# Low-rank gate products in fours on the column groups, activations held until the fourth

## The chip, the cores and the metric

The kernel runs as one program on one core of a Trainium2 chip. Its metric is device time in microseconds (us). PE is the matrix engine (TensorE) and PEld its weight loads; DVE, ACT and POOL are VectorE, ScalarE and GpSimd; SPq is the queue of SyncE, which issues most DMA transfers here.

## The reference

One layer of a diffusion backbone on 128 prompt tokens and 1024 latent tokens, D = 1024. Cut to what matters here:

```python
h = rmsnorm(x, norm1) * (1 + scale1) + shift1
q_a, k_a, v_a, g_a, lr_a, q_b, f_b, i_b, g_b = jnp.split(h @ w_in, offsets, axis=-1)
lr = lr_a.reshape(B, T, 2, GLA_LOWRANK)  # 2 x 16 = 32 of the columns of w_in
alpha_logit = jnp.einsum('btdr,drk->dbtk', lr, w_gla_up) + b_gla[:, None, None, :]
log_alpha = jax.nn.log_sigmoid(alpha_logit.astype(jnp.float32)) / GLA_GATE_NORM
```

The mixer's gated scans with `log_alpha`, its output product and a convolutional FFN follow.

## The kernel before, in words

The 1152 tokens are cut into three blocks `g` of 384 (three tiles of 128 tokens each, `xt`), taken in the order 2, 1, 0. The 1024 columns are cut into eight blocks `kt` of 128. For each `g` and `kt` the function `modulate` does this:

- three transposes on PE (L478) bring the normalised tokens into a PSUM tile `x`; there are four such tiles, in the pools `ps_o` and `ps_lv`;
- one operation takes it out of PSUM with scale and shift into the SBUF tile `tt`: on DVE (L487), or on ACT (L483) for blocks 2 and 5 of `g` 1 and 0;
- ACT makes the rounded half `h1h` (L492), POOL (even `kt`) or DVE (odd `kt`) the remainder `h1l` (L69);
- the hook `each`, here `lr_part` (L528), multiplies `tt` by the 32 low-rank columns `wlr`. Such a product fills 32 of the array's 128 columns. Its place among the four column groups, and so the 32 PSUM partitions of `plr` that it writes, is `kt % 4`.

`modulate` is called with `kt` 0 to 3 and then 4 to 7, so a block `g` has two sets of four low-rank products; the second set accumulates onto the first. The trace records each of the 24 products as two matmuls. After both calls ACT takes `plr` out (L555) and stores it in DRAM as `scr_lr`, from where a later stage loads it again as `lr` (L835) for the products with `wup` (L839).

Before a block's transposes, `norm_x` normalises each of its three tiles: a sum of squares on ACT (L378), two small steps on DVE and POOL (L379, L380), and a scaling of the tile on DVE (L385). After a block's `modulate` come projections of 24 matmuls each (L506), called here by output and block: q of block 2; k of 2 and q of 1; k of 1, q and k of 0. Then the next stage begins with L839 and the projections at L617.

The order of each engine's instructions is not written by hand here. The program is built with a scheduler that lists the instructions of an engine by its own estimate of when each is ready, and at run time each engine takes them strictly in that order. `tc.issue_after(i)` tells that scheduler to put what follows behind instruction `i`. So a change in one place can move instructions on every engine near it. Pools hand out buffers in turn: the sixth `tt` waits until the first is free.

Of the kernel before, what the change touches and what calls it, by code (L numbers as in the profile page):

```python
# [49 lines left out]
def kernel(ctx: ExitStack, tc: tile.TileContext, ins, outs, stop=None):  # L50
# [3 lines left out]
    def pool(stack, name, bufs, space=None, side=None):  # L54
        kw = {} if space is None else {"space": space}
        if side is not None:
            kw["side"] = side
        return stack.enter_context(tc.tile_pool(name=name, bufs=bufs, reuse_waits="tile", **kw))

    mm = nc.tensor.matmul  # L60
# [203 lines left out]
    def next_w():  # L264
        prefetch_w()
        while pos["used"] in stored:
            pos["used"] += 1
            prefetch_w()
        pos["used"] += 1
        return pos["got"][pos["used"] - 1]  # L270
# [22 lines left out]
    es0 = ExitStack()  # L293
    rowp = pool(es0, "rows", 1)
    wap_ = pool(es0, "wa", 12)
    xp = pool(es0, "x", 3)
    tp = pool(es0, "t", 5)

    crow = rowp.tile([16, P], F32, name="crow")
    nc.sync.dma_start(crow[0:8, :], ins["c_ctx"].rearrange("(k p) -> k p", p=P))  # L300
# [82 lines left out]
    def norm_x(t):  # L383
        st = rstd_of(tp, x_in[t], "p")
        nc.vector.tensor_scalar(x_in[t], x_in[t], st[:, 1:2], None, op0=ALU.mult)  # L385
# [3 lines left out]
    for i in range(2):  # L389
        nc.vector.memset(modA[i], 0.0)  # L390
        t = modA[i][:, :]
# [7 lines left out]
    for i in range(2):  # L399
        ps = (ps_a, ps_mm)[i].tile([2 * 32, 512], F32, name="ada", tag=("ada", "mm")[i])  # L400
        psA.append(ps)
        for kt in range(KT):
# [4 lines left out]
            for j in range(2):  # L407
# [4 lines left out]
                    start=(kt == 0),  # L412
                    stop=(kt == KT - 1),
                    skip_group_check=True,
# [9 lines left out]
    wlr = rowp.tile([P, KT, 32], F32, name="wlr")  # L424
# [14 lines left out]
    def ada_first(i):  # L439
        nc.vector.tensor_tensor(modA[i], psA[i], modA[i], op=ALU.add)  # L440
        pt = ps_x.tile([P, 4, P], F32, name="x", tag="x")
        for q in range(4):
            nc.tensor.transpose(pt[:, q, 0:64], modA[i][:, q * P : (q + 1) * P], ident[0:64, 0:64])
        nc.vector.tensor_copy(b1[i], pt[:, :, 0:2])
        for v in range(2):
            nc.vector.scalar_tensor_tensor(
                s1[i][:, :, v],
                pt[:, :, 32 + v],
                one_c[:, 0:1],
                vcol[:, col["norm1"] + 4 * i : col["norm1"] + 4 * i + 4],  # L450
                op0=ALU.add,
                op1=ALU.mult,
            )
# [18 lines left out]
    def modulate(g, xns, s, b, hi, lo, psum, tpool, lo_eng, each=None, t_act=(), kts=range(KT)):  # L472

        for kt in kts:
            pool_, tag = psum[kt % len(psum)]
            pt = pool_.tile([P, BL], F32, name="x", tag=tag)
            for i in range(3):
                nc.tensor.transpose(pt[:, i * P : (i + 1) * P], xns[i][:, kt * P : (kt + 1) * P], ident)  # L478
            t = tpool.tile([P, BL], F32, name="tt", tag="tt")
            parts = [(0, BL, 1)] if g < 2 else [(0, 2 * P, 1), (2 * P, BL, 0)]  # L480
            for c0, c1, v in parts:
                if kt in t_act:
                    nc.scalar.activation(  # L483
                        t[:, c0:c1], pt[:, c0:c1], AF.Identity, scale=s(kt, v), bias=b(kt, v)
                    )
                    continue
                nc.vector.tensor_scalar(  # L487
                    t[:, c0:c1], pt[:, c0:c1], s(kt, v), b(kt, v), op0=ALU.mult, op1=ALU.add
                )
            h_, l_ = hi(kt, g), lo(kt, g)  # L490
            for (c0, c1, hp_), (_, _, lp_) in zip(h_, l_):
                nc.scalar.activation(hp_, t[:, c0:c1], AF.Copy)  # L492
                split_lo(lo_eng[kt % len(lo_eng)], lp_, t[:, c0:c1], hp_)
            if each is not None:
                each(kt, t)
# [3 lines left out]
    def proj_d(w, b):  # L499

        hi, lo = w
        ps = ps_mm.tile([P, BL], F32, name="mm", tag="mm")
        n = 0
        for kt in range(KT):
            for a, h in ((hi, h1h), (hi, h1l), (lo, h1h)):
                mm(ps, a[:, kt, :], h[kt][b], start=(n == 0), stop=(n == 23))  # L506
                n += 1
        return ps
# [4 lines left out]
    def evac(ps, nm, scale=1.0):  # L513
        t = new_pj(nm)
        nc.scalar.activation(t, ps, AF.Copy, scale=scale)  # L515
        return t

    first_q, first_k = {}, {}
    for g in (2, 1, 0):
        if g < 2:  # L520
            for t in range(3 * g, 3 * g + 3):
                norm_x(t)
        xns = [x_in[t] for t in range(3 * g, 3 * g + 3)]
        plr = ps_mm.tile([P, BL], F32, name="mm", tag="mm")

        def lr_part(kt, t):
            j = kt % 4
            mm(  # L528
                plr[32 * j : 32 * j + 32, :],
                wlr[:, kt, :],  # L530
                t,
                start=(kt < 4),
                stop=(kt >= 4),
                skip_group_check=True,
            )

        for i in range(2):
            if g == 2 and i == 1:
                ada_first(1)
            modulate(  # L540
                g,
                xns,
                lambda k, v: s1[k // 4][:, k % 4, v : v + 1],
                lambda k, v: b1[k // 4][:, k % 4, v : v + 1],
                lambda k, g: [(0, BL, h1h[k][g])],
                lambda k, g: [(0, BL, h1l[k][g])],
                ((ps_o, "o"), (ps_lv, "lv")),
                tp,
                (nc.vector,) if g == 2 and i == 0 else (nc.gpsimd, nc.vector),
                lr_part,  # L550
                (1, 3, 5) if g == 2 else (2, 5),
                range(4 * i, 4 * i + 4),
            )
        lrs = tp.tile([P, BL], F32, name="lrs", tag="lrs", bufs=1)
        nc.scalar.activation(lrs, plr, AF.Copy)  # L555
        nc.scalar.dma_start(scr_lr[g], lrs)
        if g == 2:
            wq = next_w()
            first_q[2] = evac(proj_d(wq, 2), "qj", 0.125)
            wk = next_w()  # L560
        elif g == 1:
            first_k[2] = evac(proj_d(wk, 2), "kj")
            first_q[1] = evac(proj_d(wq, 1), "qj", 0.125)
        else:
            first_k[1] = evac(proj_d(wk, 1), "kj")
            first_q[0] = evac(proj_d(wq, 0), "qj", 0.125)
            first_k[0] = evac(proj_d(wk, 0), "kj")
# [637 lines left out]
    for n, u in enumerate(groups):  # L1205
# [7 lines left out]
        for bi, b in enumerate(ORDER):  # L1213
            fb, k, k0 = ready
            lv = levels(u, b, fb, k, k0)
            for slot in range(8):
                at = 8 * bi + slot
                last = anchor["mm"] = next(lv)
# [1095 lines left out]
def build(nc, shapes, outs_kind="ExternalOutput", stop=None):  # L2314
    ins = {
        n: nc.dram_tensor(f"in_{n}_dram", s, dt, kind="ExternalInput").ap() for n, (s, dt) in shapes.items()
    }
    outs = [
        nc.dram_tensor(f"out_{i}_dram", s, F32, kind="ExternalOutput").ap() for i, (s, _) in enumerate(_OUTS)
    ]  # L2320
    with tile.TileContext(nc, schedule_with_timeline_sim=True) as tc:
        kernel(tc, ins, outs, stop)
# [14 lines left out]
```

## Time and profile before

| | |
|---|---|
| median of 3 runs | 1548.68 us (1547.78 to 1554.11) |
| profiled execution, its own time | 1549.85 us |
| its span, first to last instruction | 1548.1 us |
| PE busy | 1487.8 us (96%), 12506 matmuls |
| DVE, ACT, POOL busy | 1145.5 us (74%), 783.2 us (51%), 708.9 us (46%) |
| low-rank products, L528 | 48 records, first at 31.7 us, last at 72.7 us |
| granted TensorE clock | 0.99 mean |

The change lies in the first 90 us of the span, so shares of the whole span say little about it. The chain of work that ended last, listed in order of time, tells which engine the end of that stretch hangs on; a timeline gives the single instructions, and a view by stretches the busy time of each engine in a window.

### The profile page before, as it was taken

Reading aid. Unit: us, or ns where it says so; the run is one execution under the profiler, and the core shown is the slowest. Engines: PE = TensorE matmul, PEld = TensorE weight load, DVE = VectorE, ACT = ScalarE, POOL = GpSimd, SP = SyncE. Lnnn points to the kernel's source line nnn. Section 1 sums busy time; section 2 is a strip of 40 time slices with the busy share of each in tenths; the row PEclk is TensorE's granted clock in tenths of the full one; section 3 lists DMA queues with packets and bytes.
Section 4 is the critical chain, followed back from the end, with each engine's and each line's share of the span. In section 5 each row is a group of like instructions: output and inputs, shape, how many; then the busy total and the mean of one; then the engine's idle time right before and its main releaser. Section 6 shows DMA issues by size and latency. Waiting matters only on the chain.

```text
span 1548.1 us, 31132 instructions
## 1 busy us (share of the span) xinstructions
PE 1487.8 (96%) x12506; PEld 1255.0 (81%) x12506; DVE 1145.5 (74%) x1731; ACT 783.2 (51%) x1523; POOL 708.9 (46%) x538
## 2 busy tenths in 40 slices
PE   7999999999999989899989999999999999999997
PEld 2699998999898978777767888888888887788886
DVE  3657466664556757655789999999999999579575
ACT  3566567555454544512664444444444444467444
POOL 1412122334233240222227999999999996000001
PEclk9999999999999999999999999999999999999999
DMA  9311121335435362677652555545644666879752
GB/s 339 113 54 47 35 65 51 120 92 189 135 123 182 111 198 80 235 272 278 200 180 77 179 166 128 136 118 146 193 117 135 179 162 200 330 244 360 245 192 115
DMA packets 172940, 252.49 MB, mean 163 GB/s; under 512 B 11733, under 2 KB 113603, under 8 KB 170875
## 3 DMA queue, kind: packets, MB, share of 16 engines
q1 hardware_dynamic: 149591, 172.21, 34.8%
q0 software_dynamic: 22592, 77.60, 16.2%
q8 instruction: 98, 1.61, 0.4%
q10 hardware_dynamic: 611, 0.68, 0.1%
q14 instruction: 48, 0.39, 0.1%
HBM read 190.62 MB, written 82.90 MB: 177 GB/s over the span
## 4 chain that ended last, share of the span: by engine, by line
PE 78%; DMA 6%; DVE 6%; issue 4%; ACT 3%; POOL 2%; SPq 1%; POOLq 0%; ACTq 0%; DVEq 0%
PE u L1742 26%; PE mm L603 13%; PE xb L2199 6%; PE yb L2199 6%; PE mm L617 5%; PE x L1970 4%; PE mm L746 3%; PE lv L935 3%; PE yb L2250 2%; PE u L1512 2%; DVE acc L1906 2%; PE x L1003 1%; PE mm L506 1%; DMA mh<-scr_m 1%; DMA wa<-in_w_ada_dram 1%
## 5 line engine op out<-in xcount | busy, mean ns | idle before, releaser
L1906 DVE SCALAR_TENSOR_TENSOR acc<-u,convc,acc 128x945 f32<-128x945 f32 (+2 forms) x352 | 426.8, 1218 | 7.8 <-ACT acc L1894 0.7
L69 POOL TENSOR_TENSOR wl<-raw,wh 128x1024 fp32r<-128x1024 f32 x42 | 103.6, 2468 | 241.0 <-ACT wh L132 183.2
L603 PE MATMUL mm<-h1h,wh 128*128 128x384 f32 x528 | 186.0, 352 | 0.8 <-ACT qj L515 0.8
L603 PE MATMUL mm<-h1l,wh 128*128 128x384 f32 x528 | 180.0, 341 | 0.0
L603 PE MATMUL mm<-h1h,wl 128*128 128x384 f32 x528 | 180.0, 341 | 0.0
L898 DVE TENSOR_TENSOR Q<-Q,fb 128x384 f32<-128x384 f32 x126 | 86.3, 685 | 90.5 <-PE lv L935 89.0
L69 POOL TENSOR_TENSOR wul<-sr,wuh 128x512 fp32r<-128x512 f32 (+1 forms) x64 | 116.2, 1816 | 19.5 <-ACT wuh L1727 19.3
L69 POOL TENSOR_TENSOR wul<-ra,wuh 128x1024 fp32r<-128x1024 f32 x44 | 112.3, 2552 | 20.3 <-ACT wuh L1727 17.8
L888 ACT ACTIVATE m<-k 128x384 f32<-128x384 f32 x126 | 70.2, 557 | 86.9 <-PE lv L935 39.8
L2174 POOL TENSOR_TENSOR sq<-sq,mhalf 128x1 f32<-128x1 f32 x9 | 11.1, 1231 | 213.3 <-DVE sq L2171 213.3
L603 PEld LDWEIGHTS mm<-h1h,wh 128*128 128x128 f32 x528 | 100.3, 190 | 5.7 <-issue 3.9
L603 PEld LDWEIGHTS mm<-h1l,wh 128*128 128x128 f32 x528 | 100.3, 190 | 0.6 <-issue 0.2
L603 PEld LDWEIGHTS mm<-h1h,wl 128*128 128x128 f32 x528 | 100.0, 189 | 0.8 <-issue 0.5
L617 PE MATMUL mm<-wh,h1h 128*128 128x256 f32 x288 | 83.9, 291 | 0.8 <-ACT v L642 0.8
L900 DVE TENSOR_TENSOR k<-k,fb 128x384 f32<-128x384 f32 x126 | 74.2, 589 | 12.2 <-ACT m L888 6.7
L617 PE MATMUL mm<-wh,h1l 128*128 128x256 f32 x288 | 80.5, 280 | 0.0
L617 PE MATMUL mm<-wl,h1h 128*128 128x256 f32 x288 | 80.4, 279 | 0.0
L132 ACT ACTIVATE wh<-raw 128x1024 fp32r<-128x1024 f32 x50 | 53.0, 1059 | 44.0 <-PE mm L603 11.3
L2002 POOL TENSOR_TENSOR acc<-acc,acc 128x1152 f32<-128x1152 f32 x22 | 60.0, 2729 | 9.8 <-DVE acc L1906 9.8
L1727 ACT ACTIVATE wuh<-ra 128x1024 fp32r<-128x1024 f32 x42 | 44.3, 1055 | 39.5 <-issue 16.6
L1934 ACT ACTIVATE u2p<-u 128x512 f32<-128x512 f32 x44 | 26.4, 601 | 70.1 <-PE u L1742 70.1
L1727 ACT ACTIVATE wuh<-sr 128x512 fp32r<-128x512 f32 (+1 forms) x62 | 48.1, 775 | 24.1 <-PE x L1970 16.1
(387 smaller groups left out, 4485.5 us busy)
## 6 DMA issues: line engine op xcount, KB each, us to landing
ra<-in_w_ffn_up_dram SPq DMA_DIRECT2D x84, 256.0 KB, 3.0
raw<-in_w_in_dram SPq DMA_DIRECT2D x32, 512.0 KB, 4.7
v<-in_w_ada_dram SPq DMA_DIRECT2D x27, 512.0 KB, 4.3
scr_g<-acc POOLq DMA_DIRECT2D x22, 576.0 KB, 5.4
scr_s<-late POOLq DMA_DIRECT2D x11, 1024.0 KB, 5.9
scr_t<-in_w_ffn_down_dram POOLq DMA_DIRECT2D x16, 704.0 KB, 7.2
wa<-in_w_ada_dram SPq DMA_DIRECT2D x16, 512.0 KB, 6.2
scr_t<-in_w_ffn_down_dram POOLq DMA_DIRECT2D x2, 2816.0 KB, 13.5
```

The source lines that it names most:

```text
L69: return eng.tensor_tensor(out, full, hi.bitcast(F32), op=ALU.subtract)
L603: anchor["fill"] = mm(ps, a[:, kt, :], h[kt][b], start=(n == 0), stop=(n == 23))
L617: anchor["fill"] = mm(ps, h[kt][t // 3][:, ts_], a[:, kt % 4, :], start=(n == 0), stop=(n == 23))
L888: nc.scalar.activation(aps(t, 0, [[2 * h, NB], [h, 2], [1, h]]), aps(src, 0, [[2 * h, NB], [BL + h, 2], [1, h]]), AF.Copy)
L898: nc.vector.tensor_tensor(qm, qm, aps(ff_, 2 * h - 1, [[BL - h, 2], [2 * h, NB], [0, h]]), op=ALU.mult)
L900: nc.vector.tensor_tensor(km, km, aps(ff_, BL + 2 * h - 1, [[-(BL + h), 2], [2 * h, NB], [0, h]]), op=ALU.mult)
L1727: first = nc.scalar.activation(hi, raw, AF.Copy)
L1742: last = mm(dst, w_slot(c, a, x)[:, kt, :], HB[y][b][:, kt, :], start=(start and n == 0), stop=(stop and n == 11), skip_group_check=True,)
L1906: last = nc.vector.scalar_tensor_tensor(o, u3[:, r0 + dy : r1 + dy, c0 + dx : c1 + dx], wc(3 * (dy + 1) + dx + 1), o, op0=ALU.mult, op1=AL ...
L1970: last = mm(pk, HB[h]["p"][:, 4 * half + kt, :], aps(flat(W[x]), a * 512 + kt * P, [[(b - a) * 512, 2], [1, P]]), start=(half + kt + n == ...
L2002: last = nc.gpsimd.tensor_tensor(accg, accg, accu, op=ALU.mult)
L2199: anchor["down"] = mm(banks[i], w[a][:, ts_], w[b][:, 512:1024], start=(start and j == 0 and n == 0), stop=(j == NPAIR - 1 and n == 2), sk ...
```

## The change

`lr_part` no longer issues its product at once. It keeps `(kt, tt)` in a list, and when the fourth is there it issues all four, the last one first, each ordered behind the one before it. All four `tt` of a set now stay in use until then, and the pool `t` gets 7 buffers for its tiles instead of 5.

```diff
-    tp = pool(es0, "t", 5)
+    tp = pool(es0, "t", 7)
...
+        parts_lr = []
+
         def lr_part(kt, t):
-            j = kt % 4
-            mm(
-                plr[32 * j : 32 * j + 32, :],
-                wlr[:, kt, :],
-                t,
-                start=(kt < 4),
-                stop=(kt >= 4),
-                skip_group_check=True,
-            )
+            parts_lr.append((kt, t))
+            if len(parts_lr) < 4:
+                return
+            last = None
+            while parts_lr:
+                kt, t = parts_lr.pop()
+                j = kt % 4
+                with tc.issue_after(last.ins) if last is not None else nullcontext():
+                    last = mm(
+                        plr[32 * j : 32 * j + 32, :],
+                        wlr[:, kt, :],
+                        t,
+                        start=(kt < 4),
+                        stop=(kt >= 4),
+                        skip_group_check=True,
+                    )
```

Each engine runs the same instructions as before, and from the first L839 on PE, and the matching places of the other engines, they stand in the same order. Line numbers behind the edit are 9 higher: the low-rank product is L528 before and L537 after.

In the rows that follow, a number behind a name is that of a buffer: `h1h_366` to `h1h_387` are block 2 (the eight `kt` in steps of three), `h1h_365` to `_386` block 1, `h1h_364` to `_385` block 0. The first place is PE between the end of the projection q of block 2 and the start of k of block 2, where the first set of block 1 begins.

```order
 L506 MATMUL mm<-h1h_387,wl 128x384
-L478 MATMUL x<-ident,xt 128x128 x8
-L528 MATMUL mm<-tt,wlr 32x384
+L478 MATMUL x<-ident,xt 128x128 x13
+L537 MATMUL mm<-tt,wlr 32x384 x4
 L478 MATMUL x<-ident,xt 128x128 x3
 L506 MATMUL mm<-h1h_366,wh 128x384
```

The first set of block 1 now goes out at once, behind the transposes of seven of the block's eight `kt`; the other three products, and nine transposes, have left the stream of k that follows.

The second place is PE between k of block 2 and q of block 1.

```order
 L506 MATMUL mm<-h1h_387,wl 128x384
-L528 MATMUL mm<-tt,wlr 32x384
-L478 MATMUL x<-ident,xt 128x128 x2
-L528 MATMUL mm<-tt,wlr 32x384
-L478 MATMUL x<-ident,xt 128x128 x4
+L478 MATMUL x<-ident,xt 128x128 x6
+L537 MATMUL mm<-tt,wlr 32x384 x4
+L478 MATMUL x<-ident,xt 128x128 x6
 L506 MATMUL mm<-h1h_365,wh 128x384
```

The second set of block 1 stands here as a four, among the twelve transposes for the first four `kt` of block 0, and no longer reaches into the stream of q. The first set of block 0, a four before too, stands between q and k of block 1; its second set, three issues within k before, is one four behind it.

The third place is DVE around the first set of block 1, with the normalisation of tiles of blocks 1 and 0 (L379, L385) and the copies out of PSUM for the first set (L487).

```order
-L379 TENSOR_SCALAR st<-st 128x1
+L379 TENSOR_SCALAR st<-st 128x1 x2
+L385 TENSOR_SCALAR xt<-xt,st 128x1024
 L69 TENSOR_TENSOR h1l_411<-tt,h1h_387 128x384
 L379 TENSOR_SCALAR st<-st 128x1
 L385 TENSOR_SCALAR xt<-xt,st 128x1024 x2
-L379 TENSOR_SCALAR st<-st 128x1 x2
-L487 TENSOR_SCALAR tt<-x,s_0_340,b_0_342 128x384 x2
+L379 TENSOR_SCALAR st<-st 128x1
+L487 TENSOR_SCALAR tt<-x,s_0_340,b_0_342 128x384 x3
 L385 TENSOR_SCALAR xt<-xt,st 128x1024
```

One scaling of a tile has moved ahead of the remainder `h1l` and of the copies, and the set's three copies on DVE now follow each other with no scaling between them. On SP's queue the load of `wup` (L817 before, L826 after) has moved from ahead of five `xt` loads to behind the first two loads of states (L827), with the `lr` loads behind it.

## The prediction

> **What bounds the kernel now.** I read the chain that ended last first, as shares.
>
> ```profile
> PE 78%; DMA 6%; DVE 6%; issue 4%; ACT 3%; POOL 2%; SPq 1%; POOLq 0%; ACTq 0%; DVEq 0%
> ```
>
> PE carries 78% of the end, but the edit touches only 31 to 73 us of 1548, so I went on to the same chain in order of time there. Columns: start, time on the chain, what. Nine of the single products (`x2`, two records each) stand between 50.08 and 72.40; the first and the last of them are shown.
>
> ```profile
> 45.44 0.69 DVE tt L487
> 46.13 0.04 issue
> 46.17 0.83 PE mm L528 x2
> 47.01 0.48 PE x L478 x3
> 47.48 2.60 PE mm L506 x15
> 50.08 0.76 PE mm L528 x2
> ...
> 64.69 0.87 PE x L478 x8
> 65.56 0.78 PE mm L528 x8
> 66.34 0.48 PE x L478 x3
> ...
> 71.08 0.77 PE mm L528 x4
> 71.85 0.55 PE mm L506 x2
> 72.40 0.76 PE mm L528 x2
> 73.16 9.18 PE mm L506 x51
> 82.34 1.29 PE o L839 x4
> ```
>
> From 46.17 on every piece is PE, and nothing but PE. The busy time of that stretch says the same (length, then PE, PEld, DVE, ACT, POOL, granted clock, DMA, GB/s):
>
> ```profile
> 46.17:82.18 36.01, 36.01 (x188) 25.78 (x189) 18.28 (x28) 14.54 (x28) 14.85 (x12) 1.00 0.17 52
> ```
>
> PE is busy all 36.01 us at full clock, DVE for 18.28. So work taken off PE here comes off the end, as long as PE finds its inputs.
>
> **The low-rank products.** A product alone costs 0.76 us of chain (`x2`), two together 0.77 (`x4`), four together 0.78 (`x8`): four on four column groups run side by side. Between 46.17 and 73.16 the chain pays 12 slots: 0.83 + 9 x 0.76 + 0.77 + 0.78 = 9.22 us. The change leaves four fours, 4 x 0.78 = 3.12. That is **-6.1 us**. Both sets of block 2, earlier, are fours already. The fours now go out last column group first; I take their price as unchanged.
>
> The Trainium skill (TensorE: Matmul & The Clock Gate, Part 3, Measured speedup vs the span model) speaks for less: three column tiles were measured at 2.38 times one, not 3. At that efficiency of 0.79 a four would be an estimated 0.96 us and the term -5.4, the time 1543.5. Here the trace shows 0.78, and the measurement decides.
>
> **Entering and leaving.** A product among projections costs more than its slot:
>
> ```profile
> 61.72 0.34 PE L506 MATMUL mm<-h1l,wh 128*128 128x384 f32 x1
> 61.99 0.83 PE L528 MATMUL mm<-tt,wlr 128*32 128x384 f32 x2
> 62.75 0.45 PE L506 MATMUL mm<-h1h,wl 128*128 128x384 f32 x1
> 63.03 0.34 PE L506 MATMUL mm<-h1h,wh 128*128 128x384 f32 x1
> ```
>
> Projection matmuls start 0.17 us apart (2.60 / 15), but here it is 0.27 before the product and 0.28 after it: 0.2 us for one visit. Eight visits fewer are worth 0 (if transposes at the same places still pay it) to -1.6; the transposes too now come in longer runs, so I take the middle, **-0.8 us**.
>
> **First set of block 1.** PE must now hold its queue until the fourth `tt` is there, with the last transposes and the whole of k of block 2 behind it. The copies in question before, from DVE's and ACT's timelines:
>
> ```profile
> 45.44 1.26 DVE L487 TENSOR_SCALAR tt<-x,s,b 128x384 f32<-128x384 f32 x2 [0.30 <-PE x L478]
> 46.62 0.74 DVE L385 TENSOR_SCALAR xt<-xt,st 128x1024 f32<-128x1024 f32 x1
> 47.28 0.67 DVE L487 TENSOR_SCALAR tt<-x,s,b 128x384 f32<-128x384 f32 x1
> 45.94 0.66 ACT L483 ACTIVATE tt<-x,b,s 128x384 f32<-128x384 f32 x1
> ```
>
> ACT's copy is ready at 46.6 and no limit. DVE now does three copies in a row, 3 x 0.63 = 1.9, from 45.44, or up to 0.74 later for the scaling that moved ahead: done at 47.3 to 48.1. The four adds 0.78 and three transposes 0.33 (0.11 each, 0.87 / 8) to 0.48: k starts at 48.4 to 49.4, against 47.48. That is 0.9 to 1.9 late, but nine transposes (1.0 to 1.4 us) are done that stood inside k before. Net -0.5 to +0.9; I take **+0.2**.
>
> **Second set of block 1, first set of block 0.** The copies must keep ahead of PE at two more places. What DVE does in this stretch, by group (count, busy and mean ns, idle):
>
> ```profile
> L487 DVE TENSOR_SCALAR tt<-x,s,b 128x384 f32<-128x384 f32 x12 | 7.8, 673 | 4.9 <-PE x L478 4.7 <-PE mm L528 0.2
> L69 DVE TENSOR_TENSOR h1l<-tt,h1h 128x384 fp32r<-128x384 f32 x8 | 7.1, 893 | 0.4 <-ACT h1h L492 0.3
> L385 DVE TENSOR_SCALAR xt<-xt,st 128x1024 f32<-128x1024 f32 x5 | 4.7, 933 | 0.5 <-POOL st L380 0.4
> L572 DVE CAST low_masks<-mraw 32x160 uint8<-32x160 f32 x4 | 1.2, 308 | 0.0
> L570 DVE CAST masks<-mraw 128x896 uint8<-128x896 f32 x1 | 0.6, 609 | 0.0
> ```
>
> PE reaches the second set after k (24 x 0.174 = 4.2) and six transposes (0.7), so at 53.3 to 54.3. DVE has from 47.3 to 48.1 on a scaling (0.9), the mask casts (0.6 + 1.2), three copies (2.0) and one remainder (0.9): 5.6 us, done at 52.9 to 53.7. Then the last scaling of block 0, 0.9, ends at 53.8 to 54.6, while PE does the four and two transposes: no wait. PE is through q at 59.3 to 60.3 with five transposes more; DVE needs three remainders (2.7) and three copies (2.0) from 54.6 on: 59.3. The two run level, so one slow operation shows as a wait. Below, that costs nothing; above, I take at both places the nearest wait of PE for DVE, 1.46 us on a remainder:
>
> ```profile
> 41.75 0.45 PE L506 MATMUL mm<-h1l,wh 128*128 128x384 f32 x1 [1.46 <-DVE h1l L69]
> ```
>
> So 0 to 2.9; nearer the first end, since the sums come out level: **+0.8**. Before the last four stands all of k of block 1 (4.2 us), which covers the three copies (2.0) and two remainders (1.8) that are left: nothing. The two more `tt` buffers cost no time and keep the held tiles from stopping the copies.
>
> **What lies behind.** The order after the first L839 is the old one, so a PE that arrives early finds the others early as well. What could be late next comes over DMA (rows of ACT's and SP's timelines, then of the tile `wup` with the time its loads take to land):
>
> ```profile
> 73.20 0.49 ACT L555 ACTIVATE lrs<-mm 128x384 f32<-128x384 f32 x1 [4.72 <-PE mm L528]
> 75.75 1.28 SPq L835 DMA_DIRECT2D lr<-scr_lr  x3
> 66.85 0.82 SPq L827 DMA_DIRECT2D st<-in_state_gla_dram  x2
> L817 SPq DMA_DIRECT2D wup<-in_w_gla_up_pad_dram x2: 332/476/621, 31.0 to 98.5; - x2
> DMA to landing us min/median/max: 2.0/4.3/6.7
> ```
>
> `lr` was issued 2.6 us after the last product's end (73.16) and was needed at 82.34, 9.2 us after it. Now q and k of block 0, 48 x 0.18 = 8.6 us, lie between: covered. `wup`, 31.0 before, now follows the state loads, which went out at 66.85, just behind the last transposes (66.34); those come some 4 us earlier now, so it is issued at about 63.7 and lands at 66 to 70, needed at 76: covered.
>
> **The sum.** -6.1 - 0.8 + 0.2 + 0.8 = **-5.9 us**; bounds -6.1 - 1.6 - 0.5 = -8.2 and -6.1 + 0.9 + 2.9 = -2.3. The durations are from the profiled execution (1549.85 us, 1.2 above the median), which would become 1544.0; the median 1548.68 becomes **1542.8**, with 1540.5 to 1546.4 as this case's own range. About 0.5% (7.7 us) is what a measurement of this kernel can tell from no change, so the likeliest result lies within it.
>
> **Rivals.**
>
> *DVE becomes the bound (0.15).* Busy time in two stretches, columns as above:
>
> ```profile
> 46.00:54.00 8.00, 7.83 (x38) 4.73 (x38) 7.93 (x15) 4.70 (x10) 6.44 (x6) 1.00 0.19 46
> 54.00:62.00 8.00, 8.00 (x41) 5.21 (x40) 5.79 (x8) 3.10 (x6) 3.13 (x3) 1.00 0.19 57
> ```
>
> For it: DVE is full, 7.93 of 8, just where the copies are due earlier, and each four waits for the slowest copy. Against: 2.2 us are free in the next 8. If each of three sets comes 1.0 to 2.0 us late, 3 to 6 of the 6.9 gained are lost: 1545 to 1548. The Trainium skill (TensorEngine Tiling (Array Packing), Performance Considerations, PSUM Bottleneck) names this: once tiling has sped up TensorE, the copy out of PSUM may become the bottleneck. Before, it is hardly at work: from 44 to 82 us PE waited once for the input of a low-rank product (us in total, times, longest):
>
> ```profile
> PE mm L528 <- DVE tt L487: 0.4, 1, 0.4
> ```
>
> *More than the slots (0.11).* Visits cost the full 0.2 and waits nothing: -8, 1540.5, faster by just over 0.5%. For it: the short runs of L506 in the chain (0.55 for two at 71.85, against 0.35). Against: each copy must be on time.
>
> *`wup` late, slower than before (0.02).* The state loads were held by something that the trace doesn't name; if that comes after q of block 0 now, `wup` and `lr` behind it on SP's queue are late. It decides from a landing after 82.3 on, with the longest flight of 6.7 from an issue after 75.6: then L839 starts no earlier than before, and everything behind it slips. Issued at the end of k of block 0, about 76.4, it would land at 83.1: +0.8, 1549.5. Over 0.5% it is only from an issue after 83.3 on.
>
> *No overlap (0.02).* If fours in falling column order ran one after the other, 24 products would cost 0.76 each: 16 x 0.76 - 9.22 = +2.9 late and up to 2 x 2.3 in block 2: 1551.6 to 1556.
>
> **How the numbers follow.** The sum's case has 0.70. Faster by over 0.5%: 0.11, the second rival. Slower by over 0.5% (above 1556.4): 0.02, from the far ends of the last two. Within: 0.87. The range 1540.3 to 1547.6 takes in the sum's bounds and most of DVE's case; some 0.05 lie below it and 0.08 above.
>
> **What would show it.** In the profile after: 16 of the 24 products as four groups of eight records, 0.8 us each; the chain PE alone from the first of them on; k of block 2 starting at 48.4 to 49.4; the first L839 near 76 instead of 82.2; and that lead kept to the end. Wrong, if PE shows idle time before L537 put down to DVE's or ACT's `tt`, or before L839 (then of L848 in new lines) put down to a DMA, or if the lead at L839 is gone at the end.

## The result and the profile after

| | before | after |
|---|---|---|
| median of five runs, us | 1550.27 (1547.78 to 1554.11) | 1540.87 (1539.0 to 1542.7) |
| profiled execution, us | 1549.85 | 1542.7 |
| its span, us | 1548.1 | 1540.9 |
| first `wup` product (L839, now L848) starts, us | 82.2 | 76.0 |

The ratio is 0.9943, 95% interval 0.9929 to 0.9958: 0.6% faster. The profiled executions differ by 7.2 us, of which 6.2 are there at the first `wup` product.

The shares of the chain in the page of the kernel after hardly differ from those before:

```profile
PE 80%; DMA 6%; DVE 5%; ACT 3%; issue 3%; POOL 2%; SPq 1%; ACTq 0%; POOLq 0%; DVEq 0%
```

So again the chain in order of time, for the stretch that the edit touches (start, time on the chain, what):

```profile
44.70 0.94 POOL st L380
45.64 0.03 issue
45.67 0.48 DVE xt L385
46.15 0.18 issue
46.34 0.15 DVE st L379
46.48 0.59 DVE tt L487
47.08 0.04 issue
47.12 0.55 PE x L478 x3
47.67 0.04 issue
47.71 0.88 PE x L478 x6
48.59 0.78 PE mm L537 x8
49.37 0.48 PE x L478 x3
49.85 4.16 PE mm L506 x24
54.01 0.66 PE x L478 x6
54.66 0.78 PE mm L537 x8
55.45 0.80 PE x L478 x6
56.25 4.17 PE mm L506 x24
60.42 0.55 PE x L478 x5
60.97 0.78 PE mm L537 x8
61.75 0.92 PE x L478 x7
62.67 4.17 PE mm L506 x24
66.83 0.78 PE mm L537 x8
67.62 8.52 PE mm L506 x48
76.14 1.29 PE o L848 x4
```

Four fours (`x8`, 0.78 us each) stand where twelve slots stood (ten singles, a pair and a four), each projection runs its 24 matmuls in one piece, and from 47.71 on the chain is PE. The busy time of the stretch from k of block 2 to the first `wup` product confirms it (length, then PE, PEld, DVE, ACT, POOL, granted clock, DMA, GB/s):

```profile
49.85:76.14 26.29, 26.29 (x169) 23.76 (x169) 15.51 (x21) 12.07 (x25) 14.16 (x11) 1.00 0.23 69
```

PE is busy for all 26.29 us at full clock. Of the waits of PE from 45 to 76 us one is left (us in total, times, longest), on a transpose ahead of the first four; no low-rank product waits:

```profile
PE x L478 <- DVE tt L487: 1.1, 1, 1.1
```

Ahead of it the chain runs over DVE and POOL, the normalisation of blocks 1 and 0 (L380, L385, L379). It sets when the first copy (46.48) can start. On PE nine transposes stand behind that copy, and the first four behind them.

### The profile page after: what moved, and what is told of

Its sections match the earlier page's. It is cut to its first block, busy times and chain, and to the rows that moved or that the text cites. A ratio compares the mean times of both kernels' runs of the same rounds, so it can differ in the third digit from the quotient of the medians.

```text
span 1540.9 us, 31129 instructions
## 1 busy us (share of the span) xinstructions
PE 1483.3 (96%) x12506; PEld 1258.1 (82%) x12506; DVE 1147.4 (74%) x1731; ACT 783.7 (51%) x1523; POOL 710.4 (46%) x538
## 3 DMA queue, kind: packets, MB, share of 16 engines
q8 instruction: 98, 1.61, 0.4%
## 4 chain that ended last, share of the span: by engine, by line
PE 80%; DMA 6%; DVE 5%; ACT 3%; issue 3%; POOL 2%; SPq 1%; ACTq 0%; POOLq 0%; DVEq 0%
PE u L1751 26%; PE mm L612 15%; PE xb L2208 6%; PE yb L2208 6%; PE mm L626 5%; PE x L1979 4%; PE mm L755 3%; PE lv L944 3%; PE yb L2259 2%; PE u L1521 2%; PE x L1012 2%; DVE acc L1915 2%; DMA raw<-in_w_in_dram 1%; PE mm L506 1%; DMA mh<-scr_m 1%
## 5 line engine op out<-in xcount | busy, mean ns | idle before, releaser
L1736 ACT ACTIVATE wuh<-ra 128x1024 fp32r<-128x1024 f32 x42 | 44.3, 1055 | 40.1 <-issue 20.5
```

The source lines that it names most:

```text
L1736: first = nc.scalar.activation(hi, raw, AF.Copy)
```

## The experiments

Each ratio is against the kernel before on the same chip, with its 95% interval. The *early stretch* is the time from the first projection matmul (L506) to the first `wup` product (L839 or L848) in the profile: 47.8 us in the profile of before, 41.4 in that of after. It is taken from starts rounded to 0.1 us, and it is free of how the first loads fall, which moves its start by up to 2 us from one profile to the next.

### Both kernels again

The kernel after, unaltered, in two more sets:

> The changed kernel unaltered, for a second profile. Theory A (the gain is the 8 matmul slots saved on PE before the first L848): the first L848 again near 76.0 us, since everything up to there is the same work in the same order; ratio to before 0.992 to 0.997. Rival B (a good part of the measured gain is a chance of that run, DMA waits around 390 and 570 us and the clock): the first L848 near 76 too, but the lead over before at 650 us is 6 us instead of 9, and the cold stretch of the clock at 36 to 43 us is gone, with L848 1 to 2 us earlier if that stretch cost anything.

> The changed kernel unaltered, a third time. From the first L506 to the first L848 it took 41.4 and 42.0 us in two profiles, against 47.8 and 47.5 for the kernel before: 6 us. Its timed runs were 9.4 and 12 us faster. Theory E (behind L848 nothing is gained but what DMA waits and the clock give or take by chance): again 41 to 42.5 us for that stretch, and a ratio of 0.995 to 0.997, so that the mean over the three comes nearer to 0.996. Rival F (a further gain of 3 to 5 us behind L848, though the order there is the old one): ratio 0.992 to 0.9945 once more.

1537.84 against 1549.78 us, 0.9923 [0.9907, 0.9939], and 1538.71 against 1549.3, 0.9928 [0.9909, 0.9947]. Early stretches 42.0 and 41.3 us. The kernel before as its own rival:

> The kernel before, unaltered, for a second profile. So far the stretch from the first L1063 (207 us) to the last L603 (637 us) took 429.9 us in its one profile and 422 to 427 us in the profiles of five other executions. Theory D (the kernel before really is slower there): again 428 to 431 us. Rival E (that one execution was slow there by chance): 422 to 427 us. Ratio to before 0.999 to 1.001 in both.

0.9993 [0.998, 1.0006], early stretch 47.5 us. The stretch of theories D and E took 426 us this time, so the 430 of the first profile was in part chance. The early stretch repeats within 0.7 us, and the 6 us there are the change. But the timed medians fell by 9.4, 11.9 and 10.6 us, more than these 6, as rival F of the third run says. The experiments below had to explain both parts.

### Fewer slots saved

Pairs instead of fours:

```diff
-            if len(parts_lr) < 4:
+            if len(parts_lr) < 2:
```

> Products issued in twos instead of fours: on PE 8 slots stand behind 46 us instead of 12 before and 4 after (a pair costs 0.77 us as a single does). Theory A: 4 slots saved x 0.77 = 3.1 us and some visits, so the first L848 at 78.5 to 79.5 us, and the time about half way, 4 us under before (ratio 0.997). Rival C (the gain comes from the buffers and the new order of the other engines, not from the slots): L848 near 76, as with fours, or at 82.

Early stretch 45.6 us, 2.0 shorter than before; the first L848 came at 80.2 us, later than theory A has it. The time was 1541.64 us, 0.9949 [0.9934, 0.9964]. The chain has eight slots between the transposes and L848 where before has twelve (9.22 us); in order: 0.84, 0.77, 0.76, 0.76, 0.77, 0.78, 0.77 and 0.79, together 6.24.

Fours in block 1 only, the other products at once:

```diff
-            if len(parts_lr) < 4:
+            if len(parts_lr) < 4 and g == 1:
```

> Fours only in block 1, products issued one by one in blocks 2 and 0: 7 slots behind 46 us (4, 4, 3, 1, 2, 1, 1). Theory A: 5 slots saved x 0.77 = 3.9 us, the first L848 at 77.8 to 78.8 us, ratio 0.996 to 0.997. Rival C: near 76, since the order of DVE and ACT around 40 to 55 us is that of the changed kernel.

Early stretch 46.1 us: 1.5 shorter, with the first L848 at 81.2 us, again later than theory A has it. The time was 1539.96 us, 0.9942 [0.993, 0.9955]. Its chain has seven slots, together 5.39 us, so 3.8 less than before. But the first four starts 15.6 us after the first projection, against 13.9 in the kernel after. Most of that is the clock of PE in this one profile, which is about half for 3.5 us while PE is on the chain (the busy time as above, granted clock third from the end, and the chain there):

```profile
45.30:48.80 3.50, 3.50 (x13) 3.02 (x13) 2.53 (x6) 0.80 (x2) 1.82 (x3) 0.51 0.30 97
```

```profile
45.30 1.06 PE x L478 x4
46.36 1.61 PE mm L506 x5
```

Five projection matmuls take 1.61 us there, against 0.87 at 0.174 each, and the four transposes 1.06 against some 0.6. So an estimated 1.2 us of this early stretch belongs to the execution and not to the kernel, and the edit's own gain in it is nearer to 2.7 us than to 1.5.

In both kernels the early gain is smaller than the slots that were saved, since the first set goes out later (for pairs 13.2 us after the first projection, 11.7 before). The total goes the other way: both are 6 to 8 us better than their early stretch explains (nearer to 7 than to 8 for the second, by the estimate).

### Does the early gain reach the end?

The kernel after with k of block 0 computed three times over (48 extra matmuls), on PE's path just before L848:

```diff
-            first_k[0] = evac(proj_d(wk, 0), "kj")
+            first_k[0] = evac(proj_d(wk, 0, 3), "kj")
```

(`proj_d` repeats its loop over `kt`, and the last pass gives the value.)

> The changed kernel with the projection k of block 0 computed three times into the same tile: 48 matmuls more on PE just before the first L848, 48 x 0.174 = 8.3 us. Theory A (what is won or lost on PE before L848 passes to the end one to one): first L848 at 84.3 to 85.7 us and the time 8.3 us over the changed kernel's, about 1547.5, so a ratio to before of 0.998 to 0.9995. Rival E (the end depends on how DMA transfers meet the chain later, and a shift is swallowed or doubled): the time moves by less than 5 or more than 12 us.

Its chain has, in place of the 8.52 us for 48 matmuls:

```profile
68.48 16.84 PE mm L506 x96
```

8.3 us more. The time was 1547.22, 0.9986 [0.9973, 0.9998]; the unburdened kernel of the same set below (all remainders on DVE) took 1538.78: 8.4 us less. That kernel is not quite the kernel after; against the kernel after in its three sets, each by its difference to before, the loss is 8.5 to 11.0 us. One of the twelve executions with the extra matmuls took 3717 us, which the record does not explain; the median does not hang on it. So theory A holds: what PE gains or loses ahead of L848 reaches the end about one to one.

### What holds the first set of block 1

The kernel after with all remainders `h1l` of block 2 on DVE, none on POOL, which also does L380 on the chain above. Those of the block's first set are on DVE already, so the edit moves two remainders (`kt` 4 and 6), not the four of the expectation:

```diff
-                (nc.vector,) if g == 2 and i == 0 else (nc.gpsimd, nc.vector),
+                (nc.vector,) if g == 2 else (nc.gpsimd, nc.vector),
```

> The changed kernel with all remainders h1l of block 2 on DVE, so that POOL is free for the remainder of the second weight and for the small steps of the normalisation around 38 to 46 us. Behind the first L848 the order is unchanged. Theory G (k of block 2 starts 2 us late because DVE and POOL hold each other up at 38 to 42 us): k starts 1 us or more earlier than 49.6, ratio 0.990 to 0.993. Rival: DVE, with four more remainders, is later, and k starts at 50 us or later; ratio 0.993 to 0.996.

0.9939 [0.9927, 0.9951], early stretch 41.2 us. k of block 2 starts 14.7 us after the first projection, against 15.0, 15.7 and 14.9 in three profiles of the kernel after. In the span that is 50.2 us, so theory G failed and the rival's figures came. Moving this work did not free the first set; POOL's L380 and DVE's L385 still stand in the chain ahead of it (45.79 and 46.37 us).

### The buffers alone, and the fours without them

Single products, as before, with 7 and with 6 buffers for `tt`:

```diff
-    tp = pool(es0, "t", 5)
+    tp = pool(es0, "t", 7)
```

> The kernel before with 7 buffers in the pool t and nothing else: 12 slots still stand on PE behind 46 us, but other instructions move and the load of wup goes behind the states as in the changed kernel. Theory A: no gain, the first L839 at 81.5 to 82.7 us, ratio 0.999 to 1.001. Rival C: 78 us or earlier and a ratio under 0.998.

> The kernel before with 6 buffers in the pool t: single products as before, three of them and a few transposes a place earlier or later, everything behind the first L839 in the old order, wup unmoved. Two things have so far gone with a further gain of 3 to 6 us behind L848 that no profile places: more than 5 buffers, or products in fours. Theory A: first L506 to first L839 in 47 to 48 us, as before, and no gain there. If the buffers go with the further gain: ratio 0.996 to 0.998. If the fours do: 0.999 to 1.001.

1544.39 us, 0.997 [0.9958, 0.9981], and 1543.67, 0.9973 [0.9961, 0.9986]. The early stretches are *longer* than before, 48.5 and 49.2 us. So more buffers, with single products, make the kernel faster by 5 us, behind L839. With 7 the order of some instructions near 650 us differs as well; with 6 it is the old one from L839 on.

The fours with 5 buffers, twice, and with 6:

```diff
-    tp = pool(es0, "t", 7)
+    tp = pool(es0, "t", 5)
```

> Products in fours, but 5 buffers in the pool t as before; behind the first L848 every engine's order is that of the kernel before, and the load of wup stays ahead of the xt loads. On PE 4 slots stand behind 46 us as with 7 buffers, but the first set waits behind more transposes. Theory A (the slots make the gain): 5 to 6 us earlier at the first L848 than before, ratio 0.994 to 0.997. Rival F (7 buffers or the moved load of wup make a gain of 3 to 6 us behind 207 us, as the 7 buffers alone seemed to): ratio 0.996 to 0.998, and 428 to 431 us between the first L1063 and the last L603 (in new lines L1072 and L612).

> Fours with 5 buffers once more. The first time it took 44.3 us from the first L506 to the first L848, 3.4 under before, and its ratio was 0.9973, which is 4.2 us: nothing further. If that was no chance, again 0.9965 to 0.998; if it was, and fours as such bring a further gain: 0.994 to 0.996.

> Products in fours with 6 buffers in the pool t; the load of wup stays where it was before, and behind the first L848 the order is that of the kernel before. On PE the first set of block 1 waits behind 17 transposes as with 5 buffers, the later sets stand among the transposes of block 0. Theory A: 43 to 45 us from the first L506 to the first L848, 3 to 5 us under before. Theory E: the ratio shows these 3 to 5 us alone, 0.9965 to 0.998. Rival F in the form that 7 buffers and the moved load of wup make the further gain: the same ratio here, but 0.992 to 0.9945 in the run with 7 beside it; in the form that the fours make it: 0.994 to 0.996 here.

With 5: 1545.12, 0.9973 [0.9961, 0.9986] and 1545.71, 0.9981 [0.9968, 0.9993]; early stretches 44.3 and 44.2 us, 3.4 shorter than before where 5 to 6 were expected. With 6, `wup` stands where it stood before on SP's queue: 1539.56, 0.9942 [0.9925, 0.996], early stretch 42.9. The gain is thus not from the moved `wup`.

With 5 buffers the copies stop for held tiles, and DVE gets into the chain ahead of q of block 1. In order of time, fours with 5 buffers:

```profile
51.67 0.68 DVE tt L487
...
55.33 1.37 DVE h1l L69
56.70 0.60 DVE tt L487
...
58.27 3.40 PE mm L506 x18
```

PE waited twice for a `tt` to come out of PSUM, on transposes that need the tile. The wait of 1.2 us ahead of the first four is much the one that the kernel after has too (1.1); the second, ahead of q of block 1, is new:

```profile
57.34 0.55 PE L478 MATMUL x<-ident,xt 128*128 128x128 f32 x3 [1.44 <-DVE tt L487]
```

With two waits of 0.4 us behind it (a projection for ACT's copy of k, a product for its `tt`) that is 2.2 us. Half of the early gain is lost (44.3 instead of 41.4), most of it so. So the two buffers do belong to the change.

### The second part: taken apart, and partly placed

Every kernel, by medians of its set and by the early stretch of its profile (47.65 us is the mean of the two profiles of before); the rest is the first difference less the second:

| kernel | `tt` buffers | median less before, us | early stretch less 47.65 | rest | first to third `scr_m` store |
|---|---|---|---|---|---|
| before (profile) | 5 | | +0.1 | | 13.4 |
| before again | 5 | -1.8 | -0.1 | -1.7 | 12.2 |
| fours | 5 | -3.0 | -3.3 | +0.3 | 13.0 |
| fours, again | 5 | -2.7 | -3.4 | +0.7 | 13.3 |
| singles | 6 | -4.8 | +1.6 | -6.3 | 10.0 |
| fours | 6 | -9.7 | -4.7 | -5.0 | 10.0 |
| singles | 7 | -5.4 | +0.9 | -6.2 | 10.0 |
| after | 7 | -9.4 | -6.2 | -3.2 | 11.5 |
| after, again | 7 | -11.9 | -5.6 | -6.3 | 10.9 |
| after, once more | 7 | -10.6 | -6.3 | -4.2 | 11.5 |
| pairs | 7 | -8.1 | -2.0 | -6.1 | 10.0 |
| block 1 only | 7 | -9.8 | -1.5 | -8.3 | 10.0 |
| k three times | 7 | -0.9 | +2.1 | -3.0 | 10.0 |
| remainders on DVE | 7 | -9.3 | -6.4 | -2.9 | 10.0 |

The rest is near zero with 5 buffers (-0.2 in the mean of three) and -5.1 in the mean of the ten rows with 6 or 7, whatever their products do. It goes with the number of buffers, not with the fours. A single row says less: the kernel before against itself has -1.7, and each early stretch is that of one profile.

The last column says where part of it lies. Some 540 us into the span ACT rounds parts of the mixer's output (`hi`, L1099, 1108 with the edit) and POOL stores each pair of `hi` and `on` in `scr_m` (L1103, 1112). Three pairs follow each other in 13.0 us on average with 5 buffers and in 10.4 with more; the two groups do not overlap. The waits of ACT from 540 to 556 us, before:

```profile
ACT on L1047 <- DMA scr_m<-hi: 5.2, 1, 5.2
ACT hi L1099 <- DMA scr_m<-hi: 3.5, 1, 3.5
```

and with single products and 6 buffers, where no store is waited for (in the kernel after one such wait is left, 3.1 us):

```profile
ACT on L1047 <- PE ada L1172: 3.2, 1, 3.2
ACT hi L1099 <- DVE on L1089: 1.6, 1, 1.6
```

The first pair of stores in the two kernels, from POOL's timelines (before, then singles with 6 buffers), and how long these two took to land:

```profile
542.85 0.62 POOL L1103 DMA_DIRECT2D scr_m<-hi  x1 [4.34 <-ACT hi L1099]
543.47 0.54 POOL L1103 DMA_DIRECT2D scr_m<-on  x1
DMA to landing us min/median/max: 4.8/4.8/4.9
```

```profile
543.57 0.62 POOL L1103 DMA_DIRECT2D scr_m<-hi  x1 [4.05 <-ACT hi L1099]
544.19 0.54 POOL L1103 DMA_DIRECT2D scr_m<-on  x1
DMA to landing us min/median/max: 2.6/3.4/4.3
```

Before, both stores take 4.8 us or more; with 6 buffers the first is there after some 2.6 and the second after 4.3. So in all profiles: with 5 buffers the quicker store of the pair takes at least 4.3 us (4.8, 4.3, 4.5, 4.3), with 6 or 7 at most 2.9. ACT takes a buffer back from such a store, and waits for it. The wait counts: in all four profiles with 5 buffers the chain that ended last passes through one of these stores, for 3.5 to 4.6 us (before):

```profile
551.08 4.26 DMA scr_m<-hi
```

In none of the ten with more buffers does it; there the chain is PE's work at this place.

One more thing goes with the number of buffers in every profile: when SP sends out the next 512 KB load of `v`, behind the first `hi` store (before, then singles with 6 buffers):

```profile
542.92 0.37 SPq L1162 DMA_DIRECT2D v<-in_w_ada_dram  x1
```

```profile
543.94 0.37 SPq L1162 DMA_DIRECT2D v<-in_w_ada_dram  x1
```

That is 0.07 us behind the store before and 0.37 us with 6 buffers; in all, 0.07 to 0.10 us with 5 and 0.35 to 0.39 with more. The load and the stores are under way together, so the 0.3 us may be what decides how the stores land. No run tests it.

Shown: the rest comes with the sixth buffer, and 2.6 us of the 5 lie, in the profiles, at these stores. Open: why the number of `tt` buffers, long out of use by then, shifts the load against the stores and changes how these land; and where the other 2 to 3 us of the timed runs are. Each profile is one execution, and two of the same kernel differ by 5 us behind the first `wup` product (1465.9 and 1460.8 us to the end, before and before again). By the profiles alone that stretch takes 1464.4 us in the mean with 5 buffers and 1460.9 with more, and the two groups overlap (1460.8 to 1467.9 and 1456.2 to 1466.1); no second place stands out.

## Why the prediction was right or wrong

- **Result.** 1540.87 us lies in the range, 1.9 below the forecast and near "more than the slots" (1540.5). The 0.6% are just over the bound of 0.5%, so "within" was the wrong likeliest case. The sum itself was right for what it described: -5.9 forecast, -6.2 at the first `wup` product. With these 6.2 alone the median would be 1544.1, within 0.5% of before: the other 3.2 us, which bring it so near to "more than the slots", go with the buffers and not with that rival's reason, since the visits gained 0.8 and not 1.6 us. That is luck.
- **Slots, -6.1.** Right. Behind the start of k of block 2 low-rank products took 8.39 us of the chain before and take 2.34 now: -6.05. The falling column order costs nothing, 0.78 a four, so "no overlap" did not come. Nor did the estimate of 0.96 by the Trainium skill (TensorE: Matmul & The Clock Gate, Part 3, Measured speedup vs the span model).
- **Entering and leaving, -0.8.** Right: the 120 L506 of that part of the chain went from 21.8 us to 21.02.
- **First set of block 1, +0.2.** Right in kind, somewhat small. k starts at 49.85 against 47.48, 2.4 late where 0.9 to 1.9 was forecast, and the transposes behind that place take 1.74 us less of the chain, nine of them gone and the others in longer runs: +0.6 net. The step that fell short is the start of the three copies: the normalisation chain over POOL and DVE (L380, L385, L379) holds the first of them to 46.48, where the forecast had 45.44 to 46.2. And PE waits for that first copy, not for the last: nine transposes, 1.5 us, stand between it and the four.
- **Waits at the next two places, +0.8.** Too high: none. "The two run level" was right to be wary, though: with 6 buffers one such wait is there (1.3 us, on the second four), with 5 one of 1.4 and two of 0.4 us. The rival "DVE becomes the bound" thus came true only without the two buffers.
- **`wup`.** It went out at 70.1 and not at 63.7, just ahead of the `lr` loads and not at once behind the state loads (SP's timeline, after):

```profile
62.70 0.81 SPq L836 DMA_DIRECT2D st<-in_state_gla_dram  x2
70.13 0.33 SPq L826 DMA_DIRECT2D wup<-in_w_gla_up_pad_dram  x1
70.55 1.33 SPq L844 DMA_DIRECT2D lr<-scr_lr  x3
```

  What held it is in the waits of SP's queue from 60 to 76 us, a term that the forecast did not have. It waited for the store `scr_lr` of the last block, which ACT sends out only after the last four:

```profile
SPq L826 <- DMA scr_lr<-lrs: 6.5, 1, 6.5
```

  It was still in time, landing in 2.1 us, as PE did not wait at L848, but with less margin than the text had.
- **What lies behind, 0.** The step that failed. "The order after the first L839 is the old one, so a PE that arrives early finds the others early as well" holds, and the extra matmuls show it, but it does not make the rest equal: the same text gave the two buffers "no time", and more than five buffers go with 3 to 8 us behind L839, 5 in the mean of the ten rows. Of that the profile of before showed only ACT's waits for two stores (5.2 and 3.5 us), some 470 us behind the edit, and nothing in it ties them to the buffers.

## What to carry to other kernels

Small products that fill a quarter of the array's columns cost a full slot each; hold their inputs and issue four together where PE is the chain, and price them by the slot. Give the held tiles their own buffers: with the old number half of the early gain was lost, most of it in waits for copies. An edit of a pool's size is a change of its own, to be tried alone, even where the order of instructions stays the same.

## What the runs showed of the hardware

Four fp32 products of 128 x 32 by 384 on the four column groups take 0.78 us of the chain, one takes 0.76, also when issued from the last column group to the first.

The granted clock of PE falls to half for some us at places that differ between executions of the same kernel. From 38 to 42 us (columns as above, granted clock third from the end) before and before again, the same kernel, show:

```profile
38.00:42.00 4.00, 2.54 (x15) 1.94 (x14) 3.84 (x4) 3.98 (x8) 4.00 (x3) 1.00 1.03 409
```

```profile
38.00:42.00 4.00, 4.00 (x19) 3.75 (x16) 3.29 (x2) 3.98 (x8) 4.00 (x4) 0.58 1.03 409
```

PE was not on the chain there, so it cost little. In the profile of fours in block 1 only, PE carried the chain when it came (0.51 from 45.3 to 48.8 us), and that one profile would have misled by an estimated 1.2 us.
